# Mixer B's input projection: value and GLU gate side by side in 512-column slabs, and the turned chunk in the convolution's own PSUM banks

## The chip, the cores and the metric

The kernel runs on one core of one Trainium2 chip. The metric is the device time of one execution in microseconds (us), lower is better. A core has a matrix engine (TensorE, "PE" in the profile; its weight loads are "PEld"), a vector engine (VectorE, "DVE"), an activation engine (ScalarE, "ACT"), a general engine (GpSimd, "POOL") and a queue engine (SyncE, "SP") that here issues the weight transfers. Each engine works through its own list of instructions in order; semaphores tie the lists together. PSUM is the memory that PE writes its results to, in eight banks of 512 fp32 columns on 128 partitions.

## The reference

A trunk of four layers over 256 tokens of width 2048, mixers A, B, C, A. Only mixer B is touched:

```python
proj = h @ w_in                                    # 256 x 2048 times 2048 x 6144
val, glu_gate, gate = jnp.split(proj, 3, axis=-1)  # 2048 columns each
u = val * jax.nn.sigmoid(glu_gate)
u_pad = jnp.pad(u, ((0, 0), (30, 0), (0, 0)))
c = depthwise_conv_along_the_tokens(u_pad, conv_w) + conv_b     # 31 taps per channel
mu = c.mean(-1); var = ((c - mu) ** 2).mean(-1)
cn = (c - mu) * lax.rsqrt(var + EPS) * ln_w + ln_b
y = (silu(cn) * silu(gate)) @ w_out
```

## The kernel before

**Pieces.** All weights come as 368 slabs ("pieces") of 1 MB, in a fixed order. For each piece the main loop (L1109) writes into the engines' lists: the piece's matmuls (`p.mm`), then `cut(i + 2)`, then a `prep` and an `after` if the piece has one, then some queued side work. `cut` splits a slab that has landed into a rounded high part `wh` (ACT, L1103) and a rest `wl` (L1104), and issues the load of the slab three further on. `wl` is DVE's in most pieces and POOL's in pieces 6 to 45 of layer B (`lo`, L902). Raw slab, `wh` and `wl` have three buffers each, so `wh` of piece i+2 waits until PE has done piece i-1. A product is three fp32r matmuls: xh*wh, xh*wl, xl*wh.

**Layer B** has 48 pieces of input projection (counted 0 to 47 in this text; piece 0 is the first of layer B) and 16 of output projection. The 2048 channels are eight chunks of 256, numbered 0 to 7.

- Chunks 0 to 3 (`NARROW_PAIRS`) come as slabs of 8 contraction tiles x 256 columns: two pieces for the GLU gate, two for the value (`mm_xs2`, L189 to L204, 48 matmuls of 256 columns a piece). One PSUM bank holds both token halves.
- Chunks 4 to 7 come two at a time as slabs of 4 contraction tiles x 512 columns: four pieces for two chunks' GLU gates, four for their values (`mm_xs`, L206, 24 matmuls of 512 columns a piece). One bank per token half.
- Then 16 pieces of the output gate (`after_gate`), 512 columns wide.

`after_glu` writes the sigmoid (L726). `after_val` puts into the queue `slow` the product `m_` (L736, DVE) and one `t_` per chunk. `t_` turns the chunk to channels-on-partitions with four PE transposes into a bank from `ps_acc` and an ACT copy into `u` (L719, L720), and only then calls `conv(c)`.

**Convolution.** `conv(c)` appends 31 steps to the queue `side`. Step 0 takes two banks and starts the sums on ACT (L766); each further step is two DVE instructions (L768). Chunks with an odd number use the two `ps_t` banks, those with an even number the two `ps_s` banks. Behind step 16 a step without cost puts the statistics of the chunk before (`moments`, POOL) into the queue `rare`. `moments(3)` queues `mean` (L802 to L807: two matmuls with `ones` into a `ps_acc` bank, an ACT copy to `shift`) and six stages that use `shift`.

**Queues.** At the end of a piece the loop takes steps from `side` until their costs have used up the piece's budget (step 0 costs 0.1, other taps 0.78; the budget is 4.7 in pieces 0 to 31, 5.5 in 32 to 43, 10 in 44 to 47), and then one entry each of `slow` and `rare`, if they were there when the piece began. A step with `brk` ends the piece's turn; a step whose `need` isn't met blocks the queue.

**Tiles and banks.** `ps_acc` has four banks, `ps_s` and `ps_t` two each. Banks are handed out in the order in which the program asks for them. Whoever gets a used bank waits for the last access of the tile that had it, also where that access stands later in the program, on another engine's list.

**End of the convolution.** Behind the last tap of chunk 7 come `st1` (what is left of `rare`, then `sq1(7)` on DVE and `sq2(7)` on ACT), `st2` (column sums on PE, L834), `st3` (mean and deviation) and ten normalising groups that make the output projection's left operand.

Of the kernel before, what the change touches and what calls it, by code (L numbers as in the profile page):

```python
# [10 lines left out]
F32 = mybir.dt.float32  # L11
# [21 lines left out]
NARROW_PAIRS = 4  # L33
# [21 lines left out]
def tile_hybrid_trunk(ctx: ExitStack, tc, x, positions, norm_w, final_norm_w, a_w_in, a_w_out,  # L55
# [133 lines left out]
    def mm_xs2(np_, p, kts, hold, xs):  # L189

        def f(wh, wl):
            if p == 0:
                hold["ps"] = [ps_acc()]
            kk = len(kts)
            for t in range(2):
                for i in range(kk):
                    ps = hold["ps"][0][:, t * 256:(t + 1) * 256]
                    xh, xl = (xs(kts[i])[:, h, t * 128:(t + 1) * 128] for h in range(2))
                    T.matmul(ps, xh, wh[:, i, :], start=p == 0 and t == 0 and i == 0, stop=False,  # L199
                             skip_group_check=True)  # L200
                    T.matmul(ps, xh, wl[:, i, :], start=False, stop=False, skip_group_check=True)  # L201
                    T.matmul(ps, xl, wh[:, i, :], start=False, stop=p == np_ - 1 and i == kk - 1,  # L202
                             skip_group_check=True)
        return f  # L204

# [25 lines left out]
    def chunk_ws(w, c0, nk, after, xs=x_of, kt0=0, before=None, lo=lambda p: "v", budget=3.0, hold=None,  # L231
                 mm=None):
        hold = {} if hold is None else hold
        mm = mm or mm_wj
        np_ = nk // 8
        for p in range(np_):
            kts = list(range(p * 8, p * 8 + 8))
            pieces.append(Piece(wslab(w, kt0 + p * 8, 8, c0, 256), 8, 256, mm(np_, p, kts, hold, xs),
                                after=(lambda: after(hold["ps"])) if p == np_ - 1 else None,
                                before=before if p == 0 else None, lo=lo(p), budget=budget))  # L240

    def group_ws(w, c0, nk, after, xs, before=None, budget=3.0, lo=lambda p: "v"):

        holds = [{}, {}]
        np_ = nk // 4
        for p in range(np_):
            kts = list(range(p * 4, p * 4 + 4))
            for e in range(2):
                def done(e=e):
                    for b in range(2):  # L250
                        after(c0 // 256 + 2 * e + b, holds[e]["ps"][b])
                pieces.append(Piece(wslab(w, p * 4, 4, c0 + e * 512, 512), 4, 512,
                                    mm_ws(np_, p, kts, holds[e], xs, nb=2),
                                    after=done if p == np_ - 1 else None,
                                    before=before if p == 0 and e == 0 else None, lo=lo(p), budget=budget))
# [11 lines left out]
    def chunk_xs(w, c0, nk, after, xs=x_of, before=None, lo=lambda p: "v", budget=3.0):  # L267
        hold = {}
        np_ = nk // 4
        for p in range(np_):  # L270
            kts = list(range(p * 4, p * 4 + 4))
            pieces.append(Piece(wslab(w, p * 4, 4, c0, 512), 4, 512, mm_xs(np_, p, kts, hold, xs),
# [433 lines left out]
    def layer_b(L, wi, wo, next_layer):  # L706
# [4 lines left out]
        def tok(ps, t):  # L711
            return ps[t] if len(ps) == 2 else ps[0][:, t * 256:(t + 1) * 256]

# [8 lines left out]
        def after_glu(c, n):  # L722
            def f(ps):
                sg = lt([128, 2, 512], F32, "sg", 2)[:, :, :256 * n]
                for t in range(2):
                    A.activation(sg[:, t], tok(ps, t), AF.Sigmoid, scale=rcol[:, t:t + 1])  # L726
                ln["sg", c] = sg
            return f

        def after_val(c, n):  # L730
            def f(ps):
                sg = ln.pop(("sg", c))

                def m_():
                    for t in range(2):
                        V.scalar_tensor_tensor(sg[:, t], tok(ps, t), rcol[:, t:t + 1], sg[:, t],  # L736
                                               op0=OP.mult, op1=OP.mult)

                def t_(e):
                    u = lt([128, 2, PAD + S], F32, "u", 5)  # L740
                    G.memset(u[:, :, 0:PAD], 0.0)
                    turn(sg[:, :, e * 256:(e + 1) * 256], u[:, :, PAD:])
                    conv(c + e, u)
# [4 lines left out]
                for e in range(n):  # L748
                    slow.append(lambda e=e: t_(e))
            return f  # L750

        def conv(c, u):
# [4 lines left out]
            def taps(k):  # L757
                def f():
# [3 lines left out]
                    for j in range(2):  # L762
                        w = bw[:, 2 * c + j, k:k + 1]
                        src = u[:, j, k:k + S]
# [32 lines left out]
        def moments(c):  # L797
# [3 lines left out]
            if c == HEAD - 1:  # L801
                def mean():  # L802
                    ps = ps_acc()
# [18 lines left out]
        def layernorm():  # L822
# [6 lines left out]
            def st2():  # L829
                ps = v3(ps_acc())  # L830
# [73 lines left out]
        for c in range(NARROW_PAIRS):  # L904
            chunk_ws(wi, 2048 + c * 256, KT, after_glu(c, 1), before=open_scope(f"b{L}") if c == 0 else None,
                     lo=lo, budget=B_BUDGET, mm=mm_xs2)
            chunk_ws(wi, c * 256, KT, after_val(c, 1), lo=lo, budget=B_BUDGET, mm=mm_xs2)
        defer_first(n0, s1, s2)
        for c in range(NARROW_PAIRS, 8, 2):
            chunk_xs(wi, 2048 + c * 256, KT, after_glu(c, 2), lo=lo, budget=B_BUDGET)  # L910
            chunk_xs(wi, c * 256, KT, after_val(c, 2), lo=lo, budget=B_BUDGET)
# [174 lines left out]
    def load(i, parts=1):  # L1086
        if i < N:
            p = pieces[i]
            raw[i] = wpool.tile([128, p.kk, p.n], F32, name="raw", tag="raw", bufs=3)
            for k in range(parts):  # L1090
                sl = slice(k * p.kk // parts, (k + 1) * p.kk // parts)
                nc.sync.dma_start(raw[i][:, sl], p.src[:, sl])
# [95 lines left out]
```

## Time and profile before

| | us |
|---|---|
| runs (three) | 2245.17, 2249.04, 2249.15 |
| median | 2249.04 |
| profiled execution, its own time | 2248.17 |
| its span, first to last instruction | 2246.4 |
| layer B: first matmul of piece 0, first of the output projection, first of layer C | 562.54, 844.87, 958.90 |

Over the whole span PE is busy for 98%, DVE for 62%, ACT for 46%, POOL for 25%. Matmuls overlap in the records, so the time of a piece is read from one start to the next, not from the durations. The page's slices show PE at full share everywhere except around one stretch, the end of layer B's convolution.

### The profile page before, as it was taken

The page shows a single profiled execution, that of the slowest core. Times are in us where ns is not written, and L with a number is a line of the kernel's source. Part 1 is how long each engine was busy: PE and PEld are TensorE (multiplying, and loading weights), DVE is VectorE, ACT ScalarE, POOL GpSimd, SP SyncE. Part 2 cuts the span into 40 slices and gives each one's busy share as a digit, 9 for nine tenths or more (in the row PEclk, how much of TensorE's full clock was granted, in tenths as well). Part 3 has the DMA queues.
Part 4 walks back from the last instruction along what each step waited for, and adds up shares of the span by engine and source line. Part 5 has one row for each costly group of instructions (what it writes and reads, how often), then busy time and mean ns, then how long its engine had stood idle before and what let it go on. Part 6 is the DMA issues. An engine that isn't in the chain of part 4 may idle for free.

```text
span 2246.4 us, 29151 instructions
## 1 busy us (share of the span) xinstructions
PE 2201.7 (98%) x12080; PEld 1907.3 (85%) x12080; DVE 1397.0 (62%) x1781; ACT 1028.5 (46%) x1049; POOL 555.7 (25%) x273
## 2 busy tenths in 40 slices
PE   8999999999999997999999999999999999999998
PEld 7788888888998887988888888888888888888886
DVE  5546666667697886565556456556566446666664
ACT  4433444455434444444544444454355333444453
POOL 3004344312488972100000000000001005334311
PEclk9999999999999998999999999999999999999999
DMA  6555555545555553555565555555555655455544
GB/s 225 187 190 185 169 169 169 167 136 185 169 188 187 170 169 132 187 187 176 176 202 173 190 186 171 191 183 177 191 169 170 203 189 187 150 169 170 172 134 143
DMA packets 301405, 395.62 MB, mean 176 GB/s; under 512 B 6614, under 2 KB 212822, under 8 KB 301268
## 3 DMA queue, kind: packets, MB, share of 16 engines
q1 hardware_dynamic: 299280, 391.14, 52.8%
q8 instruction: 95, 1.56, 0.3%
q10 hardware_dynamic: 1592, 1.93, 0.3%
q0 software_dynamic: 400, 0.67, 0.1%
q14 instruction: 38, 0.31, 0.0%
HBM read 391.63 MB, written 2.10 MB: 175 GB/s over the span
## 4 chain that ended last, share of the span: by engine, by line
PE 91%; DVE 4%; ACT 3%; issue 1%; POOL 0%; DMA 0%; DVEq 0%; ACTq 0%
PE ps_acc L175 29%; PE ps_acc L176 15%; PE ps_acc L218 12%; PE ps_acc L219 12%; PE ps_acc L220 12%; DVE wl L1104 2%; PE ps_acc L199 1%; PE ps_acc L202 1%; PE ps_acc L201 1%; ACT wh L1103 1%; PE ps_acc L156 1%; PE ps_acc L154 1%; PE ps_acc L155 1%; PE ps_t L567 1%; PE ps_t L1012 1%
## 5 line engine op out<-in xcount | busy, mean ns | idle before, releaser
L1104 DVE TENSOR_TENSOR wl<-raw,wh 128x2048 fp32r<-128x2048 f32 (+1 forms) x329 | 780.7, 2374 | 536.7 <-ACT wh L1103 534.8
L1103 ACT ACTIVATE wh<-raw 128x2048 fp32r<-128x2048 f32 (+1 forms) x371 | 703.5, 1898 | 573.1 <-PE ps_acc L220 280.1
L175 PE MATMUL ps_acc<-xhl,wh 128*128 128x512 f32 x2304 | 817.1, 399 | 0.2 <-DVE xhl L338 0.2
L176 PE MATMUL ps_acc<-xhl,wl 128*128 128x256 f32 x2304 | 644.5, 280 | 0.0
L175 PEld LDWEIGHTS ps_acc<-xhl,wh 128*128 128x128 f32 x2304 | 433.3, 188 | 101.9 <-DVE xhl L338 0.6
L218 PE MATMUL ps_acc<-wh,xhl 128*128 128x512 f32 x1152 | 453.5, 394 | 0.5 <-ACT wh L1103 0.5
L219 PE MATMUL ps_acc<-wl,xhl 128*128 128x512 f32 x1152 | 450.8, 391 | 2.8 <-DVE wl L1104 2.8
L220 PE MATMUL ps_acc<-wh,xhl 128*128 128x512 f32 x1152 | 450.3, 391 | 0.0
L176 PEld LDWEIGHTS ps_acc<-xhl,wl 128*128 128x128 f32 x2304 | 435.2, 189 | 0.4
L219 PEld LDWEIGHTS ps_acc<-wl,xhl 128*128 128x128 f32 x1152 | 217.6, 189 | 48.5 <-DVE wl L1104 4.3
L220 PEld LDWEIGHTS ps_acc<-wh,xhl 128*128 128x128 f32 x1152 | 217.5, 189 | 45.7
L218 PEld LDWEIGHTS ps_acc<-wh,xhl 128*128 128x128 f32 x1152 | 217.4, 189 | 45.6 <-ACT wh L1103 1.1
L515 POOL TENSOR_TENSOR qk<-qk,ropeA 32x512 f32<-32x512 f32 x48 | 85.0, 1772 | 590.6 <-DVE tmp L514 590.6
L1104 POOL TENSOR_TENSOR wl<-raw,wh 128x2048 fp32r<-128x2048 f32 x42 | 194.5, 4634 | 69.6 <-ACT wh L1103 53.3
L304 POOL COPY ssq<-tmp 128x512 f32<-128x512 f32 x4 | 6.0, 1498 | 826.7 <-ACT tmp L334 808.5
L175 PE MATMUL ps_acc<-z,wh 128*128 128x512 f32 x512 | 180.8, 395 | 0.0
L176 PE MATMUL ps_acc<-z,wl 128*128 128x256 f32 x512 | 144.6, 283 | 0.0
L175 PEld LDWEIGHTS ps_acc<-z,wh 128*128 128x128 f32 x512 | 96.2, 188 | 21.8
L768 DVE SCALAR_TENSOR_TENSOR ps_s<-u,bw,ps_s 128x256 f32<-128x256 f32 x232 | 91.8, 482 | 26.2 <-ACT ps_s L766 26.2
L516 POOL TENSOR_TENSOR tmp<-tmp,ropeA 32x512 f32<-32x512 f32 x48 | 102.6, 2138 | 0.0
L768 DVE SCALAR_TENSOR_TENSOR ps_t<-u,bw,ps_t 128x256 f32<-128x256 f32 x232 | 91.9, 483 | 11.1 <-ACT ps_t L766 11.1
L176 PEld LDWEIGHTS ps_acc<-z,wl 128*128 128x128 f32 x512 | 96.3, 188 | 0.2
(227 smaller groups left out, 2300.1 us busy)
## 6 DMA issues: line engine op xcount, KB each, us to landing
raw<-in_a_w_in_dram SPq DMA_DIRECT2D x159, 1024.0 KB, 5.1
raw<-in_c_w_in_dram SPq DMA_DIRECT2D x96, 1024.0 KB, 5.0
raw<-in_b_w_in_dram SPq DMA_DIRECT2D x48, 1024.0 KB, 5.2
raw<-in_c_w_out_dram SPq DMA_DIRECT2D x32, 1024.0 KB, 5.2
raw<-in_a_w_out_dram SPq DMA_DIRECT2D x16, 1024.0 KB, 5.2
raw<-in_b_w_out_dram SPq DMA_DIRECT2D x16, 1024.0 KB, 5.0
xin<-in_x_dram SPq DMA_DIRECT2D x4, 512.0 KB, 8.7
out_dram<-qk SPq DMA_DIRECT2D x8, 256.0 KB, 3.2
```

What stands on the lines that cost most here:

```text
L154: T.matmul(ps, w_h, xh, start=st, stop=False, skip_group_check=True)
L155: T.matmul(ps, w_h, xl, start=False, stop=False, skip_group_check=True)
L175: T.matmul(ps, w_h, x2, start=p == 0 and i == 0, stop=False, skip_group_check=True)
L176: T.matmul(ps[:, 0:S], w_l, x2[:, 0], start=False, stop=last and i == kk - 1, skip_group_check=True)
L218: T.matmul(ps, xh, wh[:, i, :], start=p == 0 and i == 0, stop=False)
L219: T.matmul(ps, xh, wl[:, i, :], start=False, stop=False)
L220: T.matmul(ps, xl, wh[:, i, :], start=False, stop=p == np_ - 1 and i == kk - 1)
L515: G.tensor_tensor(q[:32], q[:32], ropeA[:, 0:1].to_broadcast([32, 2, S]), op=OP.mult)
L516: G.tensor_tensor(sw, sw, ropeA[:, 1:2].to_broadcast([32, 2, S]), op=OP.mult)
L768: V.scalar_tensor_tensor(ct[:, j] if k == TAPS - 1 else acc[j], src, w, acc[j], op0=OP.mult, op1=OP.add)
L1103: A.activation(wh[:, sl], r[:, sl], AF.Copy)
L1104: (V if p.lo == "v" else G).tensor_tensor(wl[:, sl], r[:, sl], wh[:, sl].bitcast(F32), op=OP.subtract)
```

## The change

- Every chunk's value and GLU gate come side by side in one slab of 4 contraction tiles x 512 columns, 256 of each, loaded by two transfers of 512 KB. A chunk is four pieces of `mm_xs`; `mm_xs2` goes. `ps_acc` is held by two chunks at a time, two banks each.
- `after_pair` writes the sigmoid, queues `m_` in `slow`, puts the turning `t_` into `side` (cost 0.1) eight steps ahead of the queue's end, with the condition that `m_` has been issued, and calls `conv(c)` at once.
- `t_` turns into a bank of the chunk's own convolution, `ps_t` or `ps_s`. `u` has two buffers instead of five.
- `mean` takes its bank from `ps_t`, `st2` from `ps_s`; both took one of `ps_acc`.
- The row statistics `s1` and `s2` move from pieces 1 and 2 to 3 and 4.

```diff
-NARROW_PAIRS = 4
+TURN_AHEAD = 8
-    def mm_xs2(np_, p, kts, hold, xs):
...
     def chunk_xs(w, c0, nk, after, xs=x_of, before=None, lo=lambda p: "v", budget=3.0):
+        cols = c0 if isinstance(c0, tuple) else (c0,)
...
-            pieces.append(Piece(wslab(w, p * 4, 4, c0, 512), 4, 512, mm_xs(np_, p, kts, hold, xs),
+            pieces.append(Piece([wslab(w, p * 4, 4, c, 512 // len(cols)) for c in cols], 4, 512,
+                                mm_xs(np_, p, kts, hold, xs),
...
-        def after_glu(c, n):
-            def f(ps):
-                sg = lt([128, 2, 512], F32, "sg", 2)[:, :, :256 * n]
-                for t in range(2):
-                    A.activation(sg[:, t], tok(ps, t), AF.Sigmoid, scale=rcol[:, t:t + 1])
-                ln["sg", c] = sg
-            return f
-
-        def after_val(c, n):
+        def after_pair(c):
             def f(ps):
-                sg = ln.pop(("sg", c))
+                sg = lt([128, 2, 256], F32, "sgv", 3)
+                for t in range(2):
+                    A.activation(sg[:, t], ps[t][:, 256:512], AF.Sigmoid, scale=rcol[:, t:t + 1])
                 def m_():
                     for t in range(2):
-                        V.scalar_tensor_tensor(sg[:, t], tok(ps, t), rcol[:, t:t + 1], sg[:, t],
+                        V.scalar_tensor_tensor(sg[:, t], ps[t][:, 0:256], rcol[:, t:t + 1], sg[:, t],
                                                op0=OP.mult, op1=OP.mult)
-                def t_(e):
-                    u = lt([128, 2, PAD + S], F32, "u", 5)
-                    G.memset(u[:, :, 0:PAD], 0.0)
-                    turn(sg[:, :, e * 256:(e + 1) * 256], u[:, :, PAD:])
-                    conv(c + e, u)
+                    ln["val", c] = True
+                u = {}
+                def t_():
+                    u[0] = lt([128, 2, PAD + S], F32, "u", 2)
+                    G.memset(u[0][:, :, 0:PAD], 0.0)
+                    turn(sg, u[0][:, :, PAD:], ps_t if c % 2 else ps_s)
                 if c == 0:
                     m_()
                 else:
                     slow.append(m_)
-                for e in range(n):
-                    slow.append(lambda e=e: t_(e))
+                step = (0.1, t_, len(side) < TURN_AHEAD, lambda: ("val", c) in ln)
+                side.insert(max(len(side) - TURN_AHEAD, 0) if len(side) >= TURN_AHEAD else len(side), step)
+                conv(c, u)
             return f
...
                 def mean():
-                    ps = ps_acc()
+                    ps = ps_t()
...
             def st2():
-                ps = v3(ps_acc())
+                ps = v3(ps_s())
...
-        for c in range(NARROW_PAIRS):
-            chunk_ws(wi, 2048 + c * 256, KT, after_glu(c, 1), before=open_scope(f"b{L}") if c == 0 else None,
-                     lo=lo, budget=B_BUDGET, mm=mm_xs2)
-            chunk_ws(wi, c * 256, KT, after_val(c, 1), lo=lo, budget=B_BUDGET, mm=mm_xs2)
-        defer_first(n0, s1, s2)
-        for c in range(NARROW_PAIRS, 8, 2):
-            chunk_xs(wi, 2048 + c * 256, KT, after_glu(c, 2), lo=lo, budget=B_BUDGET)
-            chunk_xs(wi, c * 256, KT, after_val(c, 2), lo=lo, budget=B_BUDGET)
+        for c in range(8):
+            chunk_xs(wi, (c * 256, 2048 + c * 256), KT, after_pair(c), lo=lo, budget=B_BUDGET,
+                     before=open_scope(f"b{L}") if c == 0 else None)
+        defer_first(n0, s1, s2, 3)
...
-                nc.sync.dma_start(raw[i][:, sl], p.src[:, sl])
+                n = p.n // len(p.src)
+                for j, src in enumerate(p.src):
+                    nc.sync.dma_start(raw[i][:, sl, j * n:(j + 1) * n], src[:, sl])
```

## Rows read from the trace of the kernel before

**Rows 1.** The page's chain that ended last: share of the span by engine.

```profile
PE 91%; DVE 4%; ACT 3%; issue 1%; POOL 0%; DMA 0%; DVEq 0%; ACTq 0%
```

**Rows 2.** Busy time by stretches: length, busy us of PE, PEld, DVE, ACT, POOL, granted clock, DMA.

```profile
774.00:798.00 24.00, 24.00 (x113) 19.91 (x112) 22.58 (x58) 11.38 (x11) 24.00 (x9) 1.00 0.55 177
846.00:870.00 24.00, 16.36 (x96) 15.34 (x97) 14.38 (x16) 12.59 (x21) 11.30 (x6) 0.72 0.23 79
```

**Rows 3.** Timeline of PE in the input projection: start us, duration us, instruction, [idle before].

```profile
565.07 0.28 PE L199 MATMUL ps_acc<-wh,xhl 128*128 128x256 f32 x1
...
573.71 0.28 PE L199 MATMUL ps_acc<-wh,xhl 128*128 128x256 f32 x1
...
657.06 0.40 PE L218 MATMUL ps_acc<-wh,xhl 128*128 128x512 f32 x1
...
690.22 0.39 PE L218 MATMUL ps_acc<-wh,xhl 128*128 128x512 f32 x1
...
699.74 0.39 PE L218 MATMUL ps_acc<-wh,xhl 128*128 128x512 f32 x1
...
740.15 1.03 PE L805 MATMUL ps_acc<-lsum,ones 128*128 128x256 f32 x4
```

**Rows 4.** Timeline of DVE: the convolutions of chunk 1 and the start of chunk 6.

```profile
625.45 12.73 DVE L768 SCALAR_TENSOR_TENSOR ps_t<-u,bw,ps_t 128x256 f32<-128x256 f32 x32 [0.85 <-ACT ps_t L766]
638.09 0.88 DVE L736 SCALAR_TENSOR_TENSOR sg<-ps_acc,rcol,sg 128x256 f32<-128x256 f32 x2
638.88 10.27 DVE L768 SCALAR_TENSOR_TENSOR ps_t<-u,bw,ps_t 128x256 f32<-128x256 f32 x26
649.06 0.86 DVE L768 SCALAR_TENSOR_TENSOR big<-u,bw,ps_t 128x256 f32<-128x256 f32 x2
...
770.66 22.84 DVE L768 SCALAR_TENSOR_TENSOR ps_s<-u,bw,ps_s 128x256 f32<-128x256 f32 x58 [1.76 <-ACT ps_s L766]
```

**Rows 5.** Timeline of ACT around a first tap that follows an eviction.

```profile
769.41 0.69 ACT L890 ACTIVATE sg<-ps_acc,rcol 128x512 f32<-128x512 f32 x1 [0.57 <-PE ps_acc L220]
770.00 1.05 ACT L766 ACTIVATE ps_s<-u,bw 128x256 f32<-128x256 f32 x2
```

**Rows 6.** Line L726, the sigmoid: durations in ns, minimum, median, maximum.

```profile
L726 ACT ACTIVATE sg<-ps_acc,rcol x12: 468/475/690, 581.3 to 724.0; 128x256 f32<-128x256 f32 x8, 128x512 f32<-128x512 f32 x4
```

**Rows 7.** Timeline of PE where it starts again after waiting, end of layer B.

```profile
844.87 0.38 PE L154 MATMUL ps_acc<-big,wh 128*128 128x256 f32 x1 [3.08 <-ACT big L865]
849.23 0.58 PE L155 MATMUL ps_acc<-big,wh 128*128 128x256 f32 x1 [3.97 <-DVE big L869]
...
853.73 0.28 PE L154 MATMUL ps_acc<-big,wh 128*128 128x256 f32 x1
```

**Rows 8.** One short stretch of that: length, PE busy (matmuls), granted clock, DMA share.

```profile
850.00:852.00 2.00, 1.85 (x8) 0.50 0.00 0
```

**Rows 9.** Timeline of DVE, the last convolution (chunk 7) and what follows it.

```profile
795.71 20.50 DVE L768 SCALAR_TENSOR_TENSOR ps_t<-u,bw,ps_t 128x256 f32<-128x256 f32 x52 [1.42 <-ACT ps_t L766]
817.96 6.79 DVE L1104 TENSOR_TENSOR wl<-raw,wh 128x2048 fp32r<-128x2048 f32 x1 [1.75 <-issue]
824.67 2.43 DVE L768 SCALAR_TENSOR_TENSOR ps_t<-u,bw,ps_t 128x256 f32<-128x256 f32 x6
827.02 0.86 DVE L768 SCALAR_TENSOR_TENSOR big<-u,bw,ps_t 128x256 f32<-128x256 f32 x2
```

**Rows 10.** Timeline of ACT at the beginning of piece 44.

```profile
814.85 0.69 ACT L890 ACTIVATE sg<-ps_acc,rcol 128x512 f32<-128x512 f32 x1 [2.03 <-PE ps_acc L220]
815.44 0.62 ACT L792 ACTIVATE tmp<-tmp 128x512 f32<-128x512 f32 x1
815.96 1.91 ACT L1103 ACTIVATE wh<-raw 128x2048 fp32r<-128x2048 f32 x1
```

**Rows 11.** The page's costliest groups: busy us, mean ns, idle before.

```profile
L1104 DVE TENSOR_TENSOR wl<-raw,wh 128x2048 fp32r<-128x2048 f32 (+1 forms) x329 | 780.7, 2374 | 536.7 <-ACT wh L1103 534.8
...
L1104 POOL TENSOR_TENSOR wl<-raw,wh 128x2048 fp32r<-128x2048 f32 x42 | 194.5, 4634 | 69.6 <-ACT wh L1103 53.3
```

More of the change, by code (lines that the diff above doesn't have):

```diff
@@ L187, in joined @@
             V.tensor_tensor(dst[:, j], a, dst[:, j], op=OP.add)
-    def mm_xs2(np_, p, kts, hold, xs):
[L191 to L194, printed above, removed]
-            for t in range(2):
[L196 to L203, printed above, removed]
-        return f
     def mm_xs(np_, p, kts, hold, xs):
@@ L237, in chunk_ws @@
             kts = list(range(p * 8, p * 8 + 8))
-            pieces.append(Piece(wslab(w, kt0 + p * 8, 8, c0, 256), 8, 256, mm(np_, p, kts, hold, xs),
+            pieces.append(Piece([wslab(w, kt0 + p * 8, 8, c0, 256)], 8, 256, mm(np_, p, kts, hold, xs),
                                 after=(lambda: after(hold["ps"])) if p == np_ - 1 else None,
@@ L251, in done @@
                         after(c0 // 256 + 2 * e + b, holds[e]["ps"][b])
-                pieces.append(Piece(wslab(w, p * 4, 4, c0 + e * 512, 512), 4, 512,
+                pieces.append(Piece([wslab(w, p * 4, 4, c0 + e * 512, 512)], 4, 512,
                                     mm_ws(np_, p, kts, holds[e], xs, nb=2),
@@ L709, in layer_b @@
         HEAD = 4
-        def tok(ps, t):
-            return ps[t] if len(ps) == 2 else ps[0][:, t * 256:(t + 1) * 256]
         def turn(src, dst, bank=ps_acc):
@@ L720, in turn @@
             A.activation(dst, v3(ps), AF.Copy)
-        def after_glu(c, n):
+        def after_pair(c):
             def f(ps):
-                sg = lt([128, 2, 512], F32, "sg", 2)[:, :, :256 * n]
+                sg = lt([128, 2, 256], F32, "sgv", 3)
                 for t in range(2):
-                    A.activation(sg[:, t], tok(ps, t), AF.Sigmoid, scale=rcol[:, t:t + 1])
-                ln["sg", c] = sg
-            return f
-        def after_val(c, n):
-            def f(ps):
-                sg = ln.pop(("sg", c))
+                    A.activation(sg[:, t], ps[t][:, 256:512], AF.Sigmoid, scale=rcol[:, t:t + 1])
                 def m_():
                     for t in range(2):
-                        V.scalar_tensor_tensor(sg[:, t], tok(ps, t), rcol[:, t:t + 1], sg[:, t],
+                        V.scalar_tensor_tensor(sg[:, t], ps[t][:, 0:256], rcol[:, t:t + 1], sg[:, t],
                                                op0=OP.mult, op1=OP.mult)
-                def t_(e):
-                    u = lt([128, 2, PAD + S], F32, "u", 5)
-                    G.memset(u[:, :, 0:PAD], 0.0)
-                    turn(sg[:, :, e * 256:(e + 1) * 256], u[:, :, PAD:])
-                    conv(c + e, u)
+                    ln["val", c] = True
[4 more added lines that the diff above has]
+                    turn(sg, u[0][:, :, PAD:], ps_t if c % 2 else ps_s)
                 if c == 0:
@@ L763, in f @@
                         w = bw[:, 2 * c + j, k:k + 1]
-                        src = u[:, j, k:k + S]
+                        src = u[0][:, j, k:k + S]
                         if k == 0:
```

## The prediction

> **What bounds the kernel now.** I read the chain that ended last first: 91% of it is PE [rows 1]. Then the stretches of layer B. In the input projection PE has no gap, though POOL too is busy for all of 774 to 798 [rows 2]; a microsecond taken off PE's list there reaches the end, if nothing else becomes late. In 846 to 870 PE is busy for 16.36 us of 24 at a granted clock of 0.72 [rows 2]: there the end of the convolution sets the time, a chain that alternates between DVE and ACT, and PE waits for it [rows 7]. So layer B has two parts with different limits. The change shortens the first by making matmuls wider, and moves steps of the queues that feed both.
>
> **PE's matmuls.** At 256 columns a matmul comes every 0.120 us (565.07 to 573.71, 72 of them), at 512 every 0.2267 us (690.22 to 699.74, 42 of them) [rows 3]. A narrow piece takes 48 x 0.120 = 5.76 us, a wide one 24 x 0.2267 = 5.44. Averaged over the fifteen wide pieces 16 to 30, with their three turns at about 0.35 us taken off (an estimate: four transposes that follow each other), the wide piece is (740.15 - 657.06 - 1.05) / 15 = 5.47 us [rows 3]. Sixteen narrow pieces become wide: 16 x 0.29 = 4.6 to 16 x 0.32 = 5.1 us less; I take 4.9. The rows thus show some 13 ns a matmul on top of its columns at 2.4 GHz. The Trainium skill (TensorE: Matmul & The Clock Gate, section Back-to-back issue gap) gives for the isolated gap N/2.4 + 2.5 ns; by that a pair of narrow matmuls costs only 2.5 ns more than a wide one, the change takes off 24 x 16 x 2.5 ns = 1.0 us, and the sum below would end 3.9 us higher. The rows decide.
>
> **What stays hidden.** The same 32 transposes turn the chunks. Sixteen sigmoids of 0.475 us [rows 6] replace twelve that were partly longer, on an ACT that is idle for half of the stretch [rows 2]. Each slab is two transfers of 512 KB; they are issued three pieces (16 us) before they are needed, and the buffer they go to comes free some 9 us before that, so even a second half that came several us late would be covered; cost 0. `s1` and `s2` move two pieces back with nobody waiting earlier. For the turns I compared bank and product with their place: `m_(c)` stands in piece 4c+4 and the turns in 4, 9, 14, 19, 25, 30, 35, 39, and the convolution that had the bank before always ended several pieces earlier. No new wait there.
>
> **Where the steps of the queues go.** A convolution cost 0.1 + 30 x 0.78 = 23.5, exactly five budgets of 4.7. With its turn it costs 23.6, and in piece 8 the turn of chunk 1 is met one step before its product has been issued and blocks the rest. Stepping `side`, `slow` and `rare` through the pieces gives the first taps of chunks 0 to 7 in pieces 5, 10, 15, 21, 26, 31, 36, 41; before they were 5, 10, 15, 20, 26, 31, 35, 40. Two things follow.
>
> **The mean, the large term.** Tap 16 of chunk 4 moves from piece 28 to 29. So `moments(3)` runs in piece 30 and `mean` in 31; before, in 29 and 30. In piece 31 the taps 26 to 30 of chunk 4 use 3.9 of 4.7, and tap 0 of chunk 5 (cost 0.1) still fits. `side` is served before `rare`, so chunk 5, an odd one, asks for both `ps_t` banks, and then `mean` asks for a third tile of that pair. Before, `mean` had a bank of `ps_acc` and waited for nobody. Now PE must wait until the first of chunk 5's two sums has been read for the last time: tap 30. These taps need nothing that stands behind `mean`: chunk 5 is turned in piece 30, and the only other thing among them, `m_(7)`, reads sums that PE finished with piece 31. So it is a wait and not a deadlock, and it lasts as long as DVE needs.
>
> How long: chunk 1's convolution has the same mix, 58 taps, one product of 2 x 256 columns and the first half of the last tap, and takes from 625.45 to 649.06 + 0.43 = 24.0 us [rows 4]. It begins after the last matmul of piece 31, one sigmoid and the first tap on ACT. For chunk 6 that was 769.41 to 770.66 = 1.25 us [rows 4, 5], now with a sigmoid of 0.475 instead of 0.69 us [rows 5, 6]: 1.0. DVE is free by then, since the taps of chunk 4 (24 us from piece 26 on) end about 6 us earlier. PE thus stands for 1.0 + 24.0 = 25.0 us; bounds 23.5 (DVE starts at once) to 26.5.
>
> Queued behind: PE's pieces 32 onwards; on ACT `shift` and behind it `wh` of piece 34; on POOL `wl` of 34; on SP the loads of later slabs. Pieces 32 and 33 are already split, 10.9 us of matmuls, and `shift`, `wh` and `wl` of 34 need about 0.4 + 1.91 + 4.63 = 6.9 us [rows 10, 11], so nothing further is late. DVE has then nothing to do until chunk 6's first tap, which stands in piece 36 on ACT: its lead isn't turned into anything.
>
> When PE starts again after a wait, matmuls run at a granted clock of 0.50 (1.2 GHz) [rows 8] until the last ones before 853.73, 4.5 us from 849.23 [rows 7]. That is about 2.0 us lost (half of 4 to 4.5 us, with the mean itself in it); bounds 1.2 to 3.
>
> **The end of the convolution.** Chunk 7 starts one piece later, and when `wl` of piece 46 comes on DVE's list (piece 44), taps 21 to 30 are behind it instead of 27 to 30: 12 instructions more. Before, DVE was through with tap 26 at 816.20 and waited for `wh` [rows 9, 10]; so six taps fewer ahead of it gain nothing, and six more behind it cost 12 x 0.394 = 4.7 us (58 in 22.84 us [rows 4]). `wh` comes 0.5 us earlier, because the square that stood ahead of it (L792 [rows 10]) is now behind: net 4.2, I take 4.1. Everything after hangs on the last tap: before it ended at 827.88 [rows 9], the column sums waited for it, and the chain to the output projection starts there. Bounds: `wl` of piece 46 took 6.79 us beside POOL's additions where a split takes 2.4 in the mean [rows 9, 11]; should the collision go, that takes back 4.4, so -0.3. Above, 4.7 and another slow restart: 6.7. I take the middle since POOL has the same additions there.
>
> **Sum.** -4.9 + 25.0 + 2.0 + 4.1 = +26.2 us. Against the profiled execution 2248.17 + 26.2 = 2274.4; the median of the runs is 0.9 above it, so **2275 us**. The bounds added up give 2268 to 2283.
>
> **Rivals.**
> - *No wait at the mean.* If `mean` came ahead of chunk 5's first tap, or the pool gave it a bank otherwise, the large term goes: -4.9 + 4.1 = -0.8, 2248. For it: one tap more or less in the 31 pieces before would decide it. Against: the costs are sums of constants, and the same stepping of the kernel before puts `mean` behind piece 30 and chunk 1's product behind its tap 16, where the trace has them [rows 3, 4] (32 instructions ahead of the product).
> - *The whole gain arrives* (the other side, faster): no wait, and the end doesn't move because the six taps are absorbed, as they would be if DVE's `wl` of piece 46 lost its collision with POOL. -4.9 - 0.3, 2244. It decides from the point where `wl` takes under 2.7 us.
> - *POOL falls behind as well.* From piece 32 on POOL has 12 splits at 4.63 and 13 additions or subtractions of some 1.25 us (an estimate from the window in which it is full [rows 2]) in 12 pieces instead of 13. My steps leave at least 1.3 us before each piece that needs a `wl`. If those run out, each piece takes POOL's 5.9 us instead of PE's 5.45 and a turn of 0.35 in half of them: 12 x 0.3 = 3.6 us, and with a second clock drop 6: 2281. For it: POOL has no gap in 774 to 798 [rows 2]. Against: after the wait it starts level.
> - *The change does not do what it says*, the slabs stay as costly because side-by-side transfers arrive late: +0 instead of -4.9 with the wait still there, 2280. Slack of several us speaks against.
>
> **How the numbers follow.** Forecast 0.77; no wait 0.10; whole gain 0.03; POOL behind 0.06; late transfers 0.04. A measurement of this kernel can tell about 0.2% (4.5 us) from no change. Slower: 0.77 + 0.06 + 0.04 = 0.87; same: 0.10; faster: 0.03. The forecast's bounds 2268 to 2283 contain the last two rivals. They are the ends of four terms at once, but the wait could also be shorter than its bound if DVE gets a start that I don't see, so I go down to 2264; the cases left out hold 0.13 and some tail.
>
> **What would show it.** Right: the four matmuls of L805 begin about 25 us after piece 31, released by DVE's last tap on `ps_t`, PE's slices show a hole around 742 to 767, and DVE is idle after it until chunk 6; no L199 any more, and a matmul of 512 columns every 0.2267 us from piece 0; `wl` of piece 46 with 20 taps behind it. Wrong: L805 straight behind piece 31's last matmul. Then the mean's place or bank is not what I stepped out, and the time is that of the first two rivals.

## The result and the profile after

| | before | after |
|---|---|---|
| runs beside each other (four each) | 2245.17 to 2249.15, median 2248.3 | 2272.01 to 2272.51, median 2272.27 |
| ratio | | 1.0109, 95% interval 1.0093 to 1.0125 |
| span of the profiled execution | 2246.4 | 2270.2 |
| layer B: first matmul of piece 0, first of the output projection, first of layer C | 562.54, 844.87, 956.03 | 558.40, 866.52, 978.78 |

The change costs 24 us. Layer B by itself takes 420.38 us instead of 393.49, 26.89 more. The difference of the two numbers lies outside the change: in the profiled execution of after, the unchanged code ahead of layer B was through 4.14 us earlier, and the code behind it took 1.05 us longer (26.89 - 4.14 + 1.05 = 23.8, the difference of the spans). Over all the kernels below, which share that code, the start of layer B lies between 557.94 and 562.95 us, so from here on effects are read inside layer B. (The 958.90 in the table ahead of the prediction is the first matmul of layer C that the chain of waits passes through; the first of all is at 956.03. No step used it.)

The page of after, the span in 40 equal slices: busy tenths of PE, and the clock that it was granted. The fourteenth slice, 738 to 795 us, holds the hole.

```profile
PE   8999999999999597999999999999999999999998
PEclk9999999999999798999999999999999999999999
```

PE's timeline there (columns as in [rows 3]):

```profile
588.20 0.94 PE L702 MATMUL ps_s<-ident,sgv 128*128 128x128 f32 x4 [1.28 <-DVE sgv L714]
...
763.68 2.05 PE L786 MATMUL ps_t<-lsum,ones 128*128 128x256 f32 x4 [25.22 <-DVE big L749]
765.16 0.99 PE L201 MATMUL ps_acc<-wh,xhl 128*128 128x512 f32 x1
765.95 0.63 PE L202 MATMUL ps_acc<-wl,xhl 128*128 128x512 f32 x1
766.38 0.63 PE L203 MATMUL ps_acc<-wh,xhl 128*128 128x512 f32 x1
766.80 0.63 PE L201 MATMUL ps_acc<-wh,xhl 128*128 128x512 f32 x1
...
768.08 0.59 PE L201 MATMUL ps_acc<-wh,xhl 128*128 128x512 f32 x1
768.51 0.40 PE L202 MATMUL ps_acc<-wl,xhl 128*128 128x512 f32 x1
768.75 0.39 PE L203 MATMUL ps_acc<-wh,xhl 128*128 128x512 f32 x1
```

The third fence is DVE's timeline over the same hole. It is the counterpart of [rows 4]: 14 tap instructions (two make a tap), one product of two instructions, 44 more tap instructions, and the two halves of tap 30 that write `big`.

```profile
739.46 5.67 DVE L749 SCALAR_TENSOR_TENSOR ps_t<-u,bw,ps_t 128x256 f32<-128x256 f32 x14 [6.76 <-ACT ps_t L747]
745.04 0.87 DVE L714 SCALAR_TENSOR_TENSOR sgv<-ps_acc,rcol,sgv 128x256 f32<-128x256 f32 x2
745.83 17.32 DVE L749 SCALAR_TENSOR_TENSOR ps_t<-u,bw,ps_t 128x256 f32<-128x256 f32 x44
763.06 0.86 DVE L749 SCALAR_TENSOR_TENSOR big<-u,bw,ps_t 128x256 f32<-128x256 f32 x2
792.92 22.91 DVE L749 SCALAR_TENSOR_TENSOR ps_s<-u,bw,ps_s 128x256 f32<-128x256 f32 x58 [29.00 <-ACT ps_s L747]
```

`mean` (L786) has nothing to do with chunk 5: its operands are `lsum` and `ones`. What releases it is the write of `big` from `ps_t`, chunk 5's last read of the bank. It starts 0.2 us before the recorded end of that row, when the first of the two halves is through. The last row is DVE afterwards: 29 us idle until chunk 6, so its time in the hole was not turned into a lead. The restart, by stretches (length, busy us of PE, PEld, DVE, ACT, POOL, granted clock, DMA):

```profile
764.00:768.00 4.00, 4.00 (x10) 3.15 (x10) 0.00 (x0) 2.18 (x2) 0.00 (x0) 0.50 0.00 0
768.00:770.00 2.00, 2.00 (x9) 1.56 (x8) 0.00 (x0) 0.00 (x0) 1.93 (x1) 0.87 0.00 0
```

At a granted clock of 0.50, which is 1.2 GHz, a matmul of 512 columns comes every 0.425 us (766.38 to 768.08, above, four of them); later, at 1.00, every 0.2267.

The account of layer B, piece by piece of the path, from the starts of PE's instructions (the idle time before the mean counts from the recorded end of piece 31's last matmul, 738.46; the SiLU is read from ACT's rows and the last tap from DVE's):

| part of layer B | before | after | difference |
|---|---|---|---|
| matmuls and turns to the end of piece 31, without the mean | 183.27 | 180.06 | -3.21 |
| idle before the mean | 0 | 25.22 | +25.22 |
| the mean itself | 0.68 | 1.48 | +0.80 |
| piece 32 to the start of piece 44 | 68.36 | 70.17 | +1.81 |
| SiLU of piece 43 (L890, now L871) to the end of the last tap | 13.03 | 14.20 | +1.17 |
| last tap to the first matmul of the output projection | 16.99 | 16.99 | 0 |
| output projection | 111.16 | 112.26 | +1.10 |

(The SiLU of piece 43 is 0.02 us from the start of piece 44 in both, so the rows add up to 26.89.)

### The profile page after: what moved, and what is told of

It reads as the page before. It is cut to its first block, busy times and chain, and to the rows that moved or that the text cites. A ratio compares the mean times of both kernels' runs of the same rounds, so it can differ in the third digit from the quotient of the medians.

```text
span 2270.2 us, 28460 instructions
## 1 busy us (share of the span) xinstructions
PE 2197.3 (97%) x11696; PEld 1887.8 (83%) x11696; DVE 1394.3 (61%) x1785; ACT 1030.5 (45%) x1053; POOL 555.4 (24%) x273
## 4 chain that ended last, share of the span: by engine, by line
PE 90%; DVE 5%; ACT 2%; issue 2%; DMA 1%; POOL 1%; SPq 0%; DVEq 0%; ACTq 0%; POOLq 0%
PE ps_acc L175 28%; PE ps_acc L176 14%; PE ps_acc L202 13%; PE ps_acc L203 13%; PE ps_acc L201 13%; DVE wl L1083 1%; DVE ps_t L749 1%; PE ps_acc L156 1%; PE ps_acc L154 1%; PE ps_acc L155 1%; PE ps_t L553 1%; ACT wh L1082 1%; PE ps_t L989 1%; PE ps_t L536 1%; PE ps_s L520 0%
## 5 line engine op out<-in xcount | busy, mean ns | idle before, releaser
L201 PE MATMUL ps_acc<-wh,xhl 128*128 128x512 f32 x1280 | 503.3, 393 | 0.0
L202 PE MATMUL ps_acc<-wl,xhl 128*128 128x512 f32 x1280 | 499.8, 390 | 2.9 <-DVE wl L1083 2.9
L203 PE MATMUL ps_acc<-wh,xhl 128*128 128x512 f32 x1280 | 499.7, 390 | 0.0
L202 PEld LDWEIGHTS ps_acc<-wl,xhl 128*128 128x128 f32 x1280 | 241.4, 189 | 53.0 <-DVE wl L1083 3.9
L203 PEld LDWEIGHTS ps_acc<-wh,xhl 128*128 128x128 f32 x1280 | 241.0, 188 | 50.5
L201 PEld LDWEIGHTS ps_acc<-wh,xhl 128*128 128x128 f32 x1280 | 241.4, 189 | 49.7
```

Source lines behind the costliest of these rows:

```text
L201: T.matmul(ps, xh, wh[:, i, :], start=p == 0 and i == 0, stop=False)
L202: T.matmul(ps, xh, wl[:, i, :], start=False, stop=False)
```

## Experiments

**Is it the bank, the place in the queue, or something else about the mean?** Three edits, each for one of these, and one that gives the kernel before the bank of after.

The bank alone, in the changed kernel:

```diff
                 def mean():
-                    ps = ps_t()
+                    ps = ps_s()
```

> The changed kernel with one word different: the mean takes its bank from ps_s, the pair of the even chunks, instead of ps_t. Its place behind piece 31 stays. Theory (bank): the 25.2 us in front of the mean are the wait for chunk 5's last tap, and the slow restart after it goes too, some 2.6 us; the last user of ps_s is chunk 4, whose taps end about 6 us earlier. Expected 2244.5 us, with no gap over 1 us in front of the mean, and in PE's part up to the end of piece 31 the same 180.1 us from the first matmul of layer B. Rival (data): the mean waits for what it reads, or PE waits there for weights because two half slabs come late; then the bank does not matter and the time stays at 2272 us.

Measured: 2245.77 us, ratio to before 0.9989, interval 0.9979 to 0.9998. The mean follows at once on piece 31, in PE's timeline of this kernel:

```profile
741.59 0.40 PE L203 MATMUL ps_acc<-wh,xhl 128*128 128x512 f32 x1
741.83 1.03 PE L786 MATMUL ps_s<-lsum,ones 128*128 128x256 f32 x4
```

Layer B takes 392.65 us, 27.73 less than with `ps_t` and 0.84 less than before.

The place alone: the turn costs nothing in the queue, so that a chunk again costs exactly five budgets.

```diff
-                step = (0.1, t_, len(side) < TURN_AHEAD, lambda: ("val", c) in ln)
+                step = (0.0, t_, len(side) < TURN_AHEAD, lambda: ("val", c) in ln)
```

> The changed kernel with the turn's cost in the queue 0.0 instead of 0.1; no instruction is added or taken away, the mean keeps its bank in ps_t. Theory (place): stepping the queues puts the mean behind piece 30 and chunk 5's first tap into piece 31, so the order of the two is reversed and the 25 us go; also only taps 28 to 30 of chunk 7 are behind wl of piece 46, seven fewer than in the changed kernel, worth up to 7 x 0.79 = 5.5 us at the end of the convolution. Expected 2239 to 2245 us. Rival (bank alone): a mean in the pair of the odd chunks always collides with one of them; then the gap stays and the time is 2266 to 2272 us.

Measured: 2244.05 us, ratio 0.9985 (0.9975 to 0.9994), layer B 390.31 us. The mean, still from `ps_t`, stands behind piece 30 and one piece ahead of chunk 5's first tap. What it has over the bank alone, 2.34 us, lies at the end of the convolution, where 6 instructions instead of 20 stand behind the split (from the SiLU of piece 43 to the last tap 13.03 us instead of 15.33).

The length of what stands ahead of it, by leaving out half of chunk 5's taps:

```diff
             def taps(k):
                 def f():
+                    if c == 5 and 1 <= k <= 15:
+                        return
```

> The changed kernel without the taps 1 to 15 of chunk 5 (that part of the convolution is left out; the steps stay in the queue and keep their cost, so the order of everything else is the same). Theory (bank): the wait in front of the mean is DVE's time for chunk 5, so it gets shorter by 15 x 2 x 0.394 = 11.8 us, from 25.2 to 13.4, and the kernel takes 2260.5 us. Rival (a wait of fixed length, or one on something else than the taps): 25 us stay, 2272 us.

Measured: 2262.18 us, ratio 1.006 (1.0045 to 1.0075).

And the kernel before with the bank from `ps_t`:

```diff
                 def mean():
-                    ps = ps_acc()
+                    ps = ps_t()
```

> The kernel before with the mean's bank from ps_t instead of ps_acc, nothing else. There the mean stands behind piece 30, one piece ahead of chunk 5's first tap. Theory (place): the bank alone costs nothing, within 1 us of 2248.3 us. Rival (bank alone): 25 us more, 2273 us.

Measured: 2248.3 us, ratio 1.0002 (0.9992 to 1.0011), layer B 393.36 us.

The mean in PE's timeline, first with the place alone:

```profile
734.89 1.03 PE L786 MATMUL ps_t<-lsum,ones 128*128 128x256 f32 x4
```

In PE's timeline with half of the taps:

```profile
753.91 2.05 PE L788 MATMUL ps_t<-lsum,ones 128*128 128x256 f32 x4 [12.69 <-DVE big L751]
```

In PE's timeline of before with `ps_t`:

```profile
740.41 1.03 PE L805 MATMUL ps_t<-lsum,ones 128*128 128x256 f32 x4
```

So neither half is enough by itself. The bank without the late place waits for nobody (first and third row), the late place with another bank waits for nobody, and with both the wait follows the taps: 30 of the 58 instructions between the first and the last tap are gone, and the wait is 12.5 us shorter (11.8 expected). That is what a chain of instructions of 0.4 us gives, and what a cause outside the convolution would not.

**The end of the convolution: does the last tap set it?** I had booked 4.1 us here and the trace shows 1.2. A budget of 4.8 instead of 4.7 a piece moves chunk 7's taps ahead of `wl` of piece 46 ("the split" from here on) in DVE's list: in the changed kernel with the bank alone, all of the 20 instructions that were behind it, and in the kernel before, 4 of 8.

```diff
-B_BUDGET = 4.7
+B_BUDGET = 4.8
```

> The changed kernel with mean's bank from ps_s and with a budget of 4.8 instead of 4.7 a piece in pieces 0 to 31. Chunk 7's taps then all stand ahead of wl of piece 46 in DVE's list (20 instructions behind it before this edit). Theory that the place of the split in DVE's list sets the end of the convolution: from the SiLU of piece 43 to the end of the last tap some 10 us (23.6 us of taps from a first tap as now) instead of the 15.3 us of the kernel with the bank from ps_s alone; wl of piece 46 itself then comes 3 to 4 us later and PE waits up to 3 us ahead of piece 46, beside work that waits for the chain anyway. Layer B 388 to 390.5 us (392.65 with the bank alone), time 2241 to 2243.5. Rival, the end is set by what ACT and POOL still have to do and not by the last tap: layer B stays at 392 to 393, time 2245 to 2246.

> The kernel before with a budget of 4.8 instead of 4.7. By the queues' steps 2 taps instead of 4 of chunk 7 stand behind wl of piece 46, 4 instructions of 0.394 us less. Theory that the last tap sets the end: 1 to 1.6 us less in layer B (393.49 before), time 2246 to 2247.5. Rival, that the budget by itself is what makes the changed kernel with 4.8 faster: as much less here as there, 2 us or more. Rival, the end is not set by the last tap: no change, 2247.0 to 2248.5.

Measured: before with 4.8, 2246.59 us (ratio 0.9996, 0.9987 to 1.0005, no difference in the runs). In its trace the last tap ends 11.44 us behind the SiLU of piece 43 instead of 13.03, and layer B takes 391.91 us, 1.58 less: four instructions of 0.394 us, all of which arrive. The changed kernel with bank and 4.8: 2243.68 us (ratio 0.9983, 0.9974 to 0.9992), layer B 387.25, 5.4 less than with the bank alone and also less than the 388 to 390.5 expected. But there my forecast for the tap was far off. It ends 2.47 us behind that SiLU, not 10, because chunk 7 also begins a piece earlier (its first tap on ACT at 22.1 us ahead of that SiLU instead of 14.5); 12.9 us were gained on the tap and only 5.4 arrive. Behind the tap, DVE's next two instructions now set the end, in its timeline of the changed kernel with bank and 4.8:

```profile
811.14 0.86 DVE L749 SCALAR_TENSOR_TENSOR big<-u,bw,ps_t 128x256 f32<-128x256 f32 x2
812.12 6.43 DVE L1083 TENSOR_TENSOR wl<-raw,wh 128x2048 fp32r<-128x2048 f32 x1
818.47 1.78 DVE L770 TENSOR_TENSOR tmp<-big,shift 128x512 f32<-128x512 f32 x1
```

The subtraction of chunk 7's squares (L770) needs only the tap, but stands behind the split. So the last tap sets the end as long as the split is ahead of it, and the split does so where it comes last.

**Why does one and the same split take 3.84 to 7.57 us?** That was the open size: 6.79 us before [rows 9], 3.84 after, 4.97 with the bank alone, 7.57 with the place alone. DVE's timeline of after:

```profile
837.86 3.84 DVE L1083 TENSOR_TENSOR wl<-raw,wh 128x2048 fp32r<-128x2048 f32 x1 [0.61 <-ACT wh L1082]
```

POOL's timeline of after, the same time:

```profile
833.67 4.63 POOL L1083 TENSOR_TENSOR wl<-raw,wh 128x2048 fp32r<-128x2048 f32 x1
838.25 1.30 POOL L770 TENSOR_TENSOR tmp<-big,shift 128x512 f32<-128x512 f32 x1
840.29 2.56 POOL L761 TENSOR_TENSOR lsq<-lsq,tmp 128x512 f32<-128x512 f32 x1 [0.74 <-ACT tmp L773]
```

DVE's timeline of the kernel with the bank alone:

```profile
813.62 4.97 DVE L1083 TENSOR_TENSOR wl<-raw,wh 128x2048 fp32r<-128x2048 f32 x1 [0.62 <-ACT wh L1082]
```

And POOL's there:

```profile
810.56 4.62 POOL L1083 TENSOR_TENSOR wl<-raw,wh 128x2048 fp32r<-128x2048 f32 x1
815.15 1.29 POOL L770 TENSOR_TENSOR tmp<-big,shift 128x512 f32<-128x512 f32 x1
817.18 2.56 POOL L761 TENSOR_TENSOR lsq<-lsq,tmp 128x512 f32<-128x512 f32 x1 [0.74 <-ACT tmp L773]
```

The first try took POOL's statistics away (its additions of chunks 6 and 7, and the squares of 5 and 6):

```diff
-            add_to("lsum", CT[c])
+            if c < 6:
+                add_to("lsum", CT[c])
...
-            elif c >= HEAD:
+            elif c >= HEAD and c < 5:
```

> The changed kernel with mean's bank from ps_s and without part of the layer norm's statistics: POOL's additions of chunks 6 and 7 to the sum of the channels, and the squares of chunks 5 and 6, are left out. Theory that wl of piece 46 on DVE (6.79 us before, 3.84 in the changed kernel, 4.97 with the bank from ps_s) takes as long as it does because POOL's additions run beside it: now 2.3 to 3 us, and the last tap ends 1.5 to 3 us earlier behind the SiLU of piece 43 (15.3 us there), layer B 389.5 to 391.5 us, time about 2242 to 2244. Rival, another cause (the transfers, or ACT's writing beside it): wl stays at 4.5 us or more and the last tap stays within 0.7 us.

Measured: the split takes 3.76 us, between the two expectations, and the last tap ends 14.13 us behind the SiLU, 1.2 earlier. Layer B takes 389.88 us, 2.77 less than with the bank alone, but 1.47 of that lie in the output projection; the time is 2245.73, above the 2242 to 2244 expected. What was left beside the split was POOL's own split of piece 45, which I had forgotten to count, in POOL's timeline:

```profile
810.51 4.62 POOL L1084 TENSOR_TENSOR wl<-raw,wh 128x2048 fp32r<-128x2048 f32 x1
```

It ends at 815.13, and 815.13 + 2.15 is the end of DVE's split (813.52 + 3.76 = 817.28). In after POOL first pauses at 839.55 (838.25 + 1.30, above) and the split ends at 841.70; with the bank alone 816.44 and 818.59: 2.15 again, about what a split takes that has DVE to itself (2.29 for that of piece 47 in the same traces). So the guess became: DVE's split gets nothing done until POOL pauses, and then runs through while POOL's next addition waits (2.56 us in the rows instead of 1.28). Two runs try it by making POOL busy for longer. The first repeats POOL's subtraction into the same tile, the second puts two subtractions into other tiles ahead of it:

```diff
-            (eng or G).tensor_tensor(D[c], CT[c], row2(ln["shift"]), op=OP.subtract)
+            for _ in range(3 if c == 5 else 1):
+                (eng or G).tensor_tensor(D[c], CT[c], row2(ln["shift"]), op=OP.subtract)
```

> The changed kernel with mean's bank from ps_s, and POOL's subtraction of chunk 5's squares (1.29 us in the trace) done three times in a row with the same result. Theory from six traces: DVE's split of piece 46 gets nothing done while POOL works without a pause, and ends 2.15 us after POOL's first pause behind its start; so the two additional subtractions, 2 x 1.26 us, lengthen it from 4.97 to about 7.5 us, the last tap ends 2.5 us later (17.8 us behind the SiLU of piece 43 instead of 15.3) and layer B takes 394.5 to 395.5 us (392.65 there); time 2247.5 to 2249. Rival, the two engines share what they read and write: of the additional 2.5 us only a part shows, a split of 5.5 to 6.5 us and layer B 393 to 394. Rival, the length comes from something else (the transfers, the place): 5 us as there, layer B unchanged.

```diff
+            if c == 5:
+                G.tensor_tensor(ssq, CT[c], row2(ln["shift"]), op=OP.subtract)
+                G.tensor_tensor(lt([128, S], F32, "scr"), CT[c][:, 0], ln["shift"], op=OP.subtract)
             (eng or G).tensor_tensor(D[c], CT[c], row2(ln["shift"]), op=OP.subtract)
```

> The changed kernel with mean's bank from ps_s, and ahead of POOL's subtraction of chunk 5's squares two more subtractions of the same operands into tiles that nothing reads, one of 512 columns (1.26 us) and one of 256 (about 0.66 us, an estimate by its half size). Unlike the repeated subtraction into one tile, where each had to wait for the one before to finish, these three depend on nothing and follow each other without a pause. Theory that DVE's split of piece 46 gets its turn at the first point at which POOL's next instruction has to wait: it lasts 4.97 + 1.9 = 6.9 us and the last tap ends 1.9 us later than in the kernel with the bank alone (17.2 us behind the SiLU of piece 43 instead of 15.3), layer B 394 to 395 us, time 2247 to 2248.5. Rival, the turn comes after one addition or subtraction of POOL whether it pauses or not (with the repeated subtraction the split took 4.98 us): 4.3 to 5.1 us, layer B within 0.6 us of 392.65. Rival, a share each: 5.5 to 6.2 us.

Measured: the first misses. The split takes 4.98 us as without the repeats, the last tap stays at 15.34 us, layer B takes 393.51 (2247.55 us, ratio 1.0002, 0.9992 to 1.0011), 0.9 more than with the bank alone, which lies behind the last tap (17.98 us to the output projection instead of 16.99). The second hits for the split, 6.93 us, and for the last tap, at 17.30 us. Layer B is 395.64, above the 394 to 395 expected and 3.0 more than with the bank alone: the tap explains 2.0, and 1.0 lies in the output projection (2250.0 us, ratio 1.0011, 1.0002 to 1.0021). POOL's timeline with the repeats, in two windows, up to 816.75 and from there on, because a single one shows the three as one row (DVE's split runs from 813.87 to 818.86):

```profile
815.42 1.29 POOL L771 TENSOR_TENSOR tmp<-big,shift 128x512 f32<-128x512 f32 x1
816.79 4.59 POOL L771 TENSOR_TENSOR tmp<-big,shift 128x512 f32<-128x512 f32 x2
```

DVE's timeline with the other tiles:

```profile
811.01 6.93 DVE L1086 TENSOR_TENSOR wl<-raw,wh 128x2048 fp32r<-128x2048 f32 x1 [0.62 <-ACT wh L1085]
```

And POOL's there:

```profile
812.52 1.33 POOL L771 TENSOR_TENSOR ssq<-big,shift 128x512 f32<-128x512 f32 x1
813.77 0.78 POOL L772 TENSOR_TENSOR scr<-big,shift 128x256 f32<-128x256 f32 x1
814.45 1.34 POOL L773 TENSOR_TENSOR tmp<-big,shift 128x512 f32<-128x512 f32 x1
```

The first of the repeated subtractions ends at 816.71 and the second, which writes the same tile, starts at 816.79: POOL pauses for 0.08 us, DVE has its turn there, and its split ends at 818.86, 2.15 behind the pause. The other two take 4.59 us together instead of 2.6. Three that write different tiles follow each other without a gap, keep DVE out until 815.79, and the split ends at 817.94, 2.15 later. So the miss lay in taking the repeats for work without a pause; what the theory says of a pause holds in both runs, and 0.08 us of it is enough. That the second subtraction starts late because it waits for the first one's write is read from the difference of the two edits.

**The new wait of 1.28 us** at the first turn (the row of 588.20). The statistics of the rows now end in the piece behind which chunk 0's sigmoid, product and turn stand, and PE waits for that chain. DVE's timeline of after shows its end: the copy of `rcol`, released by PE's transposes L284, and the product, released by the sigmoid.

```profile
586.96 0.16 DVE L285 COPY rcol<-ps_t 128x2 f32<-128x2 f32 x1 [3.44 <-PE ps_t L284]
587.66 0.87 DVE L714 SCALAR_TENSOR_TENSOR sgv<-ps_acc,rcol,sgv 128x256 f32<-128x256 f32 x2 [0.54 <-ACT sgv L710]
```

The last kernel takes bank and budget and turns chunk 0 one piece later:

```diff
-                step = (0.1, t_, len(side) < TURN_AHEAD, lambda: ("val", c) in ln)
+                if c == 0:
+                    push(0.0, lambda: None, brk=True)
+                step = (0.1, t_, 0 < c and len(side) < TURN_AHEAD, lambda: ("val", c) in ln)
```

> The kernel with mean's bank from ps_s and budget 4.8, and chunk 0 turned one piece after its product instead of in the same piece. Theory that PE's wait of 1.28 us at the turn of chunk 0 comes from the product being issued just ahead of the turn: the wait is gone, layer B 1.0 to 1.5 us less than with the budget alone, time 2240 to 2242.5. Rival, the wait moves with the turn (DVE is late with the product because the splits of pieces 0 to 5 stand ahead of it): layer B as with the budget alone, within 0.3 us.

Measured: **2238.42 us**, ratio to before 0.9962, interval 0.995 to 0.9975, the best of all and 34 us under the change as made. The wait is gone and layer B takes 385.49 us, 1.76 less than with bank and budget. That is more than the 1.28 in the row and than the 1.0 to 1.5 expected; most of the rest is that the four transposes that had waited also ran slower. They took 0.69 us to the next matmul (588.20 to 588.89 in after). PE's timeline of this last kernel, with no wait ahead of them, 0.35 us:

```profile
591.83 0.60 PE L702 MATMUL ps_s<-ident,sgv 128*128 128x128 f32 x4
592.18 0.48 PE L201 MATMUL ps_acc<-wh,xhl 128*128 128x512 f32 x1
```

## Why the prediction was right, and where its steps were not

**The large term: right in place, cause and size.** 25.0 forecast, 25.22 measured. It begins in the piece, at the bank and behind the tap that the stepping of the queues gave, and the runs with bank or place alone confirm that both are needed. The rival without a wait described those two kernels instead: it said 2248 for this change, and they took 2245.77 and 2244.05.

**The matmuls: right.** -4.9 forecast. The account shows -3.21 with the turn of chunk 0 in it. That turn costs 1.75 (from the first matmul of piece 0 to the mean, 167.32 us with the later turn against 169.07 without), so -3.21 - 1.75 = -4.96 is left for the sixteen pieces. (With the bank alone the mean starts 179.94 us behind the first matmul of piece 0, without a wait; counted that way it is 179.94 - 183.27 - 1.75 = -5.08.) The isolated gap that the Trainium skill states (TensorE: Matmul & The Clock Gate, section Back-to-back issue gap) would have given -1.0, an estimate from the page's figure; the measurement decides for the rows.

**"No new wait there": wrong, by 1.75 us.** That step compared the place of each turn with its product and its bank, and for chunk 0 it took a product issued in the same piece to be ready. But that product waits for the sigmoid, the sigmoid for `rcol`, and that for PE's own transposes (L284), which belong to the statistics that the change moved from pieces 1 and 2 to 3 and 4. "`s1` and `s2` move two pieces back with nobody waiting earlier" was the same mistake: nobody waits earlier, but the first user comes right behind.

**The restart: 2.0 forecast, 2.6 measured** (the rows of the mean and of pieces 32 to 44 in the account), inside 1.2 to 3. PE ran at the half clock for 4.8 us, from 763.68 to 768.51, where [rows 7] had suggested 4 to 4.5.

**The end of the convolution: the mechanism right, the size not.** 4.1 forecast, 1.17 measured, inside the bounds of -0.3 to 6.7. The twelve further instructions behind the split did cost their 4.7 us (7.83 us from the end of the split to the last tap instead of 3.13) and the split began 0.6 us earlier, as forecast, but it took 3.84 us instead of 6.79. I had named that as a bound and then took the middle "since POOL has the same additions there". The same additions, but in another order: before, DVE's split (from 817.96 [rows 9]) met the last 0.9 us of POOL's split and three additions or subtractions in a row, and in after 0.4 us and one. POOL's timeline of before:

```profile
814.24 4.62 POOL L1104 TENSOR_TENSOR wl<-raw,wh 128x2048 fp32r<-128x2048 f32 x1
818.82 1.28 POOL L780 TENSOR_TENSOR lsq<-lsq,tmp 128x512 f32<-128x512 f32 x1
820.07 1.28 POOL L780 TENSOR_TENSOR lsum<-lsum,big 128x512 f32<-128x512 f32 x1
821.31 1.29 POOL L789 TENSOR_TENSOR tmp<-big,shift 128x512 f32<-128x512 f32 x1
823.34 2.56 POOL L780 TENSOR_TENSOR lsq<-lsq,tmp 128x512 f32<-128x512 f32 x1 [0.74 <-ACT tmp L792]
```

**What was not in the sum:** +1.10 in the output projection (112.26 us), unexplained. In nine of the ten kernels tried it took between 109.65 and 111.14 us, and in the one with subtractions into other tiles 112.15.

The terms together say -4.9 + 25.0 + 2.0 + 4.1 = 26.2, and layer B shows 26.89. Term by term the difference of 0.69 is -0.06 (matmuls), +1.75 (turn), +0.22 (wait at the mean), +0.61 (restart), -2.93 (end of the convolution) and +1.10 (output projection), so misses of up to 3 us cancelled: that the sum came out within 0.7 is luck. The bounds had a slip too: as written they add up to -5.1 + 23.5 + 1.2 - 0.3 = 19.3 and -4.6 + 26.5 + 3.0 + 6.7 = 31.6, or 2268 to 2281, so the 2283 is not their sum. With the bank alone the same sums predict -0.8 and layer B shows -0.84, also by cancelling: -4.96, the turn 1.75, and the end of the convolution 2.30. The medians of the runs are only 24.0 us apart. In the profiled pair the missing 3 us lie in the unchanged code around layer B; what moves that code by some us from execution to execution no run here shows.

Of the other rivals: POOL never kept PE waiting in layer B's input projection. No late transfer shows either; the two halves of a slab land 3.9 us after issue in the median (5.1 for a whole slab of 1 MB), with 16 us until they are needed.

## What to carry to other kernels

A pool that hands out banks in program order makes a tile wait for the whole life of the one before it, also for instructions that the program has just queued: before giving an unrelated short step a bank of a long chain, look whether the chain's next round is asked for ahead of it. Costs of steps that are tuned so that a chain fills a whole number of budgets are part of the schedule; here one step of 0.1 more per chunk moved the mean behind the first tap of the next convolution, and with that convolution's own bank it cost 27.7 us of layer B. When a statistic moves, follow its first user, not only whoever waits for it now.

## What the runs showed of the hardware

DVE's split of 128 x 2048 fp32 (two operands in SBUF) is kept out by POOL's work of the same kind, and ends 2.14 or 2.15 us after POOL's first pause, whenever it was issued:

| kernel | split starts | POOL first pauses | split ends | difference |
|---|---|---|---|---|
| before | 817.96 | 822.60 | 824.75 | 2.15 |
| after | 837.86 | 839.55 | 841.70 | 2.15 |
| bank alone (e1) | 813.62 | 816.44 | 818.59 | 2.15 |
| place alone (e2) | 812.70 | 818.13 | 820.27 | 2.14 |
| bank, budget, later turn (e7) | 807.99 | 812.29 | 814.44 | 2.15 |
| before with budget (e8) | 818.37 | 822.99 | 825.14 | 2.15 |
| POOL relieved (e9) | 813.52 | 815.13 | 817.28 | 2.15 |
| repeated subtraction, pause of 0.08 us (e10) | 813.87 | 816.71 | 818.86 | 2.15 |
| more subtractions, no pause (e11) | 811.01 | 815.79 | 817.94 | 2.15 |

In the three kernels that are not in the table (half of the taps, before with `ps_t`, bank and budget) it is 2.14, 2.15 and 2.14.

The taps, with an operand in PSUM, are not held up: 18 of their instructions take 7.13 us (0.396 each) with the bank alone, where POOL adds beside them, and also where POOL has nothing left to do (the run without part of its statistics). The Trainium skill (SBUF — State Buffer, sections SBUF: two separate sides and Who interferes with whom) says that a DVE instruction with two SBUF inputs contends with a GpSimd instruction that reads SBUF and that the second to be issued is blocked until the first is through. These rows agree on who contends. They differ on the length: DVE stayed out through up to four instructions of POOL in a row (in the kernel before, from 817.96 to 822.60), until POOL itself paused.

A wait of PE costs more than its length: 2.6 us behind the long one, at a granted clock of 0.50, and some 0.5 behind the one of 1.28, where the granted clock was 1.00 (588.2 to 590.2).
